# The second block's early operand is made behind the experts' additions, its weights' low halves move from GpSimd to VectorE, and its norms get a higher priority

## The chip, the cores and the metric

The kernel runs on one core of a Trainium2 chip. The metric is the device time of one execution in microseconds (us); the median of three runs of the kernel before is 1877.12 us. TensorE multiplies matrices, VectorE and ScalarE work on tiles element by element, GpSimd can do VectorE's kind of work too, and DMAs are issued from SyncE's and GpSimd's queues. In the profile these are PE (with PEld for its weight loads), DVE, ACT, POOL and SP.

## The reference

Two transformer blocks follow each other on 256 tokens of width 1024. The first one ends with a mixture of experts and an RMS norm:

```python
x = x + mod[:, 5] * _expert_choice_ffn(h2, ...)      # 16 experts, 32 tokens each
return _rmsnorm(x, final_norm_w)                     # its result is the second block's x
```

The second block has two layers. A context of 256 tokens runs beside x and gives it keys and values. Per layer of x:

```python
hx = modulate(rms_norm(x, norm1_g[l]), mod_x[0], mod_x[1])
zx = jnp.split(hx @ w_in[l], 10, axis=-1)            # ten parts of width 256 feed four mixers
x = x + mod_x[2] * token_mixers(zx, ...)             # convolution, attention, gating; then w_out
x = x + mod_x[5] * channel_mixer(modulate(rms_norm(x, norm2_g[l]), mod_x[3], mod_x[4]), w1, w2)
```

At the end stands `rms_norm(x, final_g)`. Between the blocks two norms meet: the first block's last one and the first norm of layer 0. One pass gives the row factors of both.

## The kernel before, in words

All activations are kept transposed: `xT` is 128 partitions by 8 chunks of 256 tokens. Every large product is done in three passes: weight and activation are each split into a high part (`hi`, a rounded copy that ScalarE writes) and a low part (`lo`, source minus `hi`), and TensorE adds high by high, high by low and low by high. `load_half` (L280) loads half a weight chunk (128x1024) from the stream's DMA queue into a ring of 6 raw buffers and calls `split` (L267); the subtraction runs on the engine that is handed in.

A `Stream` holds what one strand of work uses: its pools, its DMA queue, and `lo`, the engine for the low halves. The context is strand `ZF` (L1512; low halves on VectorE, loads from GpSimd's queue) and runs between the experts' matmuls. The second block's x is strand `ZC` (L1537): low halves on GpSimd (`lo=G`) in the mixers' chunks, in six halves of the output projection and in the first three chunks of the channel mixer; loads on SyncE's queue.

The experts (L1095 to L1126) end with eight additions to `xT` (L1119), one for each chunk of 128 features; behind each of them, in the last group of experts, ScalarE squares the new chunk and TensorE sums the squares (L1125). Then a Newton iteration on VectorE turns the sums into four row factors, `both` (L1130 to L1135).

`Early` (L372) lets two products of a norm start before the norm's row is known. Its operand is x times the gain, split into `preh` (ScalarE, L382) and `prel` (VectorE, L383); the row factor multiplies the product when it leaves PSUM (L415), and the shift rides along in two added columns. `product` (L392) issues the second product behind the row's transposes; `rows` (L386) copies the row. `modulate` (L360) then makes the ordinary operand, `hh` and `hlo`, chunk by chunk for all later products.

`both_norms` (L1540) serves layer 0's first norm: it multiplies the gain with the first block's final norm weight, makes the early operand in pools of strand ZC, and transposes the row out of `both`. Its `rest` (L1548) modulates and also scales `xT` itself by the first block's final norm (L1552, eight instructions). The pools of strand ZC (`cb`, `cx`, `hlx`, `ct`) are opened after the experts' pools have been closed and take over their memory. The mixers (L1256) run the two early products (chunks 1 and 0 of w_in), which give `glu`; then the 31-tap convolution by products of 32x32 (`pconv`, L1335), keys (`pk`), values (`pvv`), the query, attention in five units, and the other chunks (`zin`). `row_params` (L1141) loads the gating rows that the mixers need at L1415.

The other norms of x go through `norm` (L1487): the early operand, then `rms_rows` (L346), which squares each chunk on ScalarE (L336), adds the squares on VectorE (`acc`, L338), sums over the partitions on TensorE (L341) and runs the Newton iteration. The final norm (L1566, L1567) scales `xT` into `yo` on ScalarE and takes `rms_rows` of `xT`.

**What sets the order.** A planner orders each engine's instructions by priority (the order in the program, unless a block asks for a high priority, as `urgent`, L318, does for the Newton iteration and the row's transposes) among those that are ready by its own estimate of the time. SyncE's queue alone keeps the program's order. [...]

Of the kernel before, what the change touches and what calls it, by code (L numbers as in the profile page):

```python
# [10 lines left out]
FT = mybir.dt.float32  # L11
# [4 lines left out]
OP = mybir.AluOpType  # L16
# [9 lines left out]
RW = 1408  # L26
# [162 lines left out]
class Stream:  # L189


    def __init__(self, **kw):
        self.__dict__.update(kw)

# [11 lines left out]
def build(tc, I, out, dbg=None, upto=99):  # L206
# [22 lines left out]
    def P(n, i=0, w=None):  # L229
        o, ww = PAR[n]  # L230
        return par[:, o + i:o + (ww if w is None else i + w)]
# [113 lines left out]

    def rms_rows(Z, xt):  # L346

        return rows_of(Z, rms_of(Z, xt))

    last_row = [None]  # L350

    @urgent
    def rows_of(Z, r):

        row = Z.ms.tile([128, 512], FT, name="rrow", tag="ms")
        for a in range(2):
            last_row[0] = PE.transpose(row[:, a * 128:(a + 1) * 128], r[:, a:a + 1].to_broadcast([128, 128]), ident)  # L357
        return row[:, :T]
# [72 lines left out]
    def mod_gain(pool, mod, m, i, norm, name):  # L431
        g = pool.tile([128, 8], FT, name=name)
        V.scalar_tensor_tensor(g, mod[:, m, i * 8:i * 8 + 8], 1.0, norm, op0=OP.add, op1=OP.mult)
        return g
# [705 lines left out]

    def row_params(Z, l):  # L1141
        r = Z.big.tile([128, NROW], FT, name="rows", tag="rows", bufs=1)
        Z.dma.dma_start(r, I["rows"][l])
        return r

    def lam_of(Z, l):
# [38 lines left out]
    def v_chunk(Z, l, H, vd):  # L1185
        parts = load_split(Z, I[f"wi2_{l}"][4], Z.lo)
        ps = Z.mm.tile([128, 2, 256], FT, name="pvv", tag="mm")
        dense(ps, parts, H, True)
        evac(vd, ps)
# [66 lines left out]
    def mixers(Z, l, H, x):  # L1256
# [125 lines left out]
        if not x:  # L1382
            taps(8, 16)
        v_chunk(Z, l, H, kvd[1])
        if not x:
            taps(16, 24)
        ps = chunk(2)
# [105 lines left out]
        early.rows(row)  # L1493
        return [early, lambda: modulate(Z, xt, gain, shift, row)]

    def layer(Z, l, mod, m, x, norm1=norm):
        g1 = mod_gain(Z.h, mod, m, 1, P(f"n1_{l}"), "g1")
        H = norm1(Z, Z.x, g1, mod[:, m, 0:8], x and Z.y or None)
        Y = mixers(Z, l, H, x)
        g2 = mod_gain(Z.big, mod, m, 4, P(f"n2_{l}"), "g2")  # L1500
        out_proj(Z, I[f"wo2_{l}"], Y, mod[:, m, 16:24], eng=Z.lo, wide=x)
        H = norm(Z, Z.x, g2, mod[:, m, 24:32], x and Z.hid or None)
        mlp(Z, l, H, mod[:, m, 40:48])
# [18 lines left out]
    v_chunk(ZF, 1, H, vc[1])  # L1522
    assert not turns
    phF.close()
    phB.close()
    if upto < 6:
        return [es, es2]


    phC = ExitStack()  # L1530
    cb = phC.enter_context(tc.tile_pool(name="cb", bufs=2))
    cx = phC.enter_context(tc.tile_pool(name="cx", bufs=1))
    hlx = phC.enter_context(tc.tile_pool(name="hlx", bufs=2))
    ct_ = phC.enter_context(tc.tile_pool(name="ct", bufs=3))
    cms = phC.enter_context(tc.tile_pool(name="cms", bufs=2, space=PSUM))
    csc = phC.enter_context(tc.tile_pool(name="csc", bufs=4, space=PSUM))
    ZC = Stream(fills=1, sq="sq", raw=ringp, rawn=RW, dma=nc.sync, acc=dict(tag="hn", bufs=1), hl=itertools.cycle([hlp, hlp, hlp, hlx, hlx]), mm=fmm, ms=cms, tmp=ct_, h=cx, big=cb, hid=((cx, "hidh"), (cx, "hidl")), y=((pz, "cT"), (cx, "yl")),  # L1537
                x=xT, np=4, ahead=1, lo=G, fill=0, sc=csc, sct="sc")

    def both_norms(Z, xt, gain, shift, places):  # L1540

        gain2 = Z.h.tile([128, 8], FT, name="gain2")
        V.tensor_mul(gain2, gain, P("fn"))
        early = Early(Z, xt, gain2, shift, places)
        row = rows_of(Z, both[:, 2:4])
        early.rows(row)

        def rest():  # L1548
            H = modulate(Z, xt, gain2, shift, row)
            row1 = rows_of(Z, both[:, 0:2])  # L1550
            for k in range(KD):
                V.scalar_tensor_tensor(xt[:, k, :], xt[:, k, :], P("fn", k, 1), row1, op0=OP.mult, op1=OP.mult)  # L1552
            return H

        return [early, rest]

    for _ in range(3):
        wait = fr.tile([128, 1024], FT, name="raw", tag="raw")
# [33 lines left out]
```

## Time and profile before

| | us |
|---|---|
| runs of the kernel before | 1870.72, 1877.12, 1877.19 |
| median | 1877.12 |
| the profiled execution's own time | 1875.34 |
| its span in the trace | 1873.5 |

The profile shows one execution. Times in the trace count from the start of the span. [...] A list of waits names for each idle stretch what ended it. A line such as `acc<-acc,sq` names the tile that an instruction writes and those that it reads.

### The profile page before, as it was taken

The numbers are of one execution on the slowest core, as the hardware profiler recorded it, in microseconds if no ns is written. First come the engines' busy times: TensorE is split into PE (matmuls) and PEld (weight loads), VectorE is DVE, ScalarE is ACT, GpSimd is POOL, SyncE is SP. The second block draws the span as 40 slices with busy tenths as digits, with TensorE's granted clock in tenths as the row PEclk, the third lists the DMA queues.
The fourth block names the chain that finished last, engine by engine and source line by source line (L and its number), as shares of the span: only waits on it lengthen the run. The fifth ranks groups of instructions, "written<-read, shape, count | busy, mean of one in ns | idle before, by whom it ended". The sixth has DMA issues, their size and how long they took to land. (4 is left out here: it accounts for less than half of the span.)

```text
span 1873.5 us, 37088 instructions
## 1 busy us (share of the span) xinstructions
PE 1663.8 (89%) x15731; PEld 1327.5 (71%) x15731; DVE 992.2 (53%) x1824; ACT 626.8 (33%) x987; POOL 340.1 (18%) x348
## 2 busy tenths in 40 slices
PE   5999999787988888888887887799999999999997
PEld 3777876454665466555764565688999997789997
DVE  5666565464533432223322341656788874967564
ACT  3432332321221221112211221344554453546443
POOL 2334141200000000000000001343311136430000
PEclk7999999888898999889998989888899999999999
DMA  9666887799899999999999998432488853235561
GB/s 372 214 225 223 333 273 275 280 404 396 305 385 403 407 398 412 397 413 409 412 406 411 406 391 309 140 113 68 129 295 299 289 173 126 86 106 191 182 188 59
DMA packets 124228, 529.32 MB, mean 283 GB/s; under 512 B 13917, under 2 KB 14173, under 8 KB 123550
## 3 DMA queue, kind: packets, MB, share of 16 engines
q1 hardware_dynamic: 91086, 405.56, 57.1%
q0 software_dynamic: 32544, 119.16, 18.2%
q8 instruction: 123, 2.02, 0.4%
q10 hardware_dynamic: 432, 2.23, 0.3%
q14 instruction: 43, 0.35, 0.1%
HBM read 525.84 MB, written 1.05 MB: 281 GB/s over the span
## 5 line engine op out<-in xcount | busy, mean ns | idle before, releaser
L269 ACT ACTIVATE hi<-raw 128x1024 fp32r<-128x1024 f32 x316 | 333.0, 1057 | 743.8 <-PE oproj L312 258.6
L271 DVE TENSOR_TENSOR lo<-raw,hi 128x1024 fp32r<-128x1024 f32 x250 | 306.9, 1230 | 407.0 <-ACT hi L269 392.7
L312 PE MATMUL oproj<-hidh,hi 128*128 128x256 f32 x768 | 223.4, 291 | 3.0 <-DVE xT L911 2.9
L312 PE MATMUL oproj<-hidh,lo 128*128 128x256 f32 x768 | 221.3, 288 | 0.0
L312 PE MATMUL oproj<-hidl,hi 128*128 128x256 f32 x768 | 220.8, 288 | 0.0
L271 POOL TENSOR_TENSOR lo<-raw,hi 128x1024 fp32r<-128x1024 f32 x66 | 160.1, 2436 | 314.0 <-ACT hi L269 254.9
L312 PE MATMUL pw<-hh,hi 128*128 128x256 f32 x704 | 204.6, 294 | 2.7 <-ACT hh L367 2.3
L312 PE MATMUL pw<-hh,lo 128*128 128x256 f32 x704 | 200.0, 286 | 0.0
L312 PE MATMUL pw<-hlo,hi 128*128 128x256 f32 x704 | 195.1, 288 | 1.1 <-DVE hlo L368 1.1
L312 PEld LDWEIGHTS oproj<-hidh,hi 128*128 128x128 f32 x768 | 149.8, 195 | 19.1 <-issue 15.0
L312 PEld LDWEIGHTS pw<-hh,hi 128*128 128x128 f32 x704 | 136.8, 195 | 26.8 <-issue 20.9
L312 PEld LDWEIGHTS oproj<-hidh,lo 128*128 128x128 f32 x768 | 149.2, 194 | 5.2 <-issue 5.2
L312 PEld LDWEIGHTS oproj<-hidl,hi 128*128 128x128 f32 x768 | 149.5, 195 | 3.9 <-issue 3.9
L1065 PE MATMUL pu<-raw,xe 128*32 128x352 f32 x1024 | 108.7, 514 | 36.3 <-DMA raw<-in_wu_dram 34.7
L1065 PE MATMUL pg<-raw,xe 128*32 128x352 f32 x1024 | 106.8, 511 | 35.7 <-DMA raw<-in_wg_dram 35.4
L312 PEld LDWEIGHTS pw<-hh,lo 128*128 128x128 f32 x704 | 136.7, 194 | 1.6 <-issue 1.5
L312 PEld LDWEIGHTS pw<-hlo,hi 128*128 128x128 f32 x704 | 133.7, 195 | 5.8 <-issue 4.4
L1112 PE MATMUL pd<-raw,ht 128*32 128x128 f32 x2816 | 109.8, 281 | 20.2 <-DMA raw<-in_wd_dram 18.8
L487 DVE CUSTOM_DVE_ANT_0 raw<-raw,adarow,par 128x1024 f32<-128x1024 f32 x64 | 85.1, 1331 | 61.0 <-DMA raw<-in_ada0x_dram 41.8
L277 POOL DMA_DIRECT2D raw<-in_w_dram x64 | 33.9, 530 | 430.3 <-DVE lo L271 430.3
L1112 PEld LDWEIGHTS pd<-raw,ht 128*32 128x32 f32 x2816 | 79.1, 111 | 43.9 <-DMA raw<-in_wd_dram 22.5
L312 PE MATMUL zin<-hh,hi 128*128 128x256 f32 x272 | 85.1, 314 | 0.8 <-ACT hh L367 0.8
(459 smaller groups left out, 3363.1 us busy)
## 6 DMA issues: line engine op xcount, KB each, us to landing
raw<-in_wg_dram SPq DMA_DIRECT2D x128, 704.0 KB, 10.0
raw<-in_wu_dram SPq DMA_DIRECT2D x128, 704.0 KB, 10.3
raw<-in_wd_dram SPq DMA_DIRECT2D x128, 704.0 KB, 9.0
raw<-in_w_dram SPq DMA_DIRECT2D x128, 512.0 KB, 4.2
raw<-in_wi_dram SPq DMA_DIRECT2D x68, 512.0 KB, 5.2
raw<-in_ada_dram POOLq DMA_DIRECT2D x64, 512.0 KB, 4.9
raw<-in_w_dram POOLq DMA_DIRECT2D x64, 512.0 KB, 7.9
raw<-in_ada0x_dram POOLq DMA_DIRECT2D x32, 512.0 KB, 5.1
```

Of the source, the lines that this page charges most:

```text
L269: A.activation(hi, src, AF.Copy, scale=scale)
L271: (eng or V).tensor_sub(lo, src, hi.bitcast(FT))
L277: Z.dma.dma_start(raw[:p, :n], src)
L312: PE.matmul(ps[:, b, :], l, r, start=(n == 0), stop=(n == 47), skip_group_check=True)
L487: V.tensor_tensor_reduce(raw, raw, row, 1.0, bias[:, 16 + n:17 + n], OP.mult, OP.add, accum_out=mod[:, 0, 16 + n:17 + n])
L1065: mm = PE.matmul(ps[32 * j:32 * j + 32, :], xe[:, k, e * 32:(e + 1) * 32], raw[:, j * 352:(j + 1) * 352], start=(k == 0), stop=(k == KD - 1))
L1112: mm = PE.matmul(py[32 * j:32 * j + 32, :], hts[j][:, i, :], raw[:, n % 11 * 128:(n % 11 + 1) * 128], start=(i == 0), stop=(i == 10))
```

## The change

- **Early operand.** Layer 0's gain (`gain2`) and `Early` are made right after the context strand, before the experts' pools are closed. The high part goes where the context's x was (`pz`, tag `cT`), the low part to a new pool, `ce`, on the other side of memory. So each chunk's instructions can run as soon as the experts' addition to that chunk is done.
- **PSUM.** Two `passed` tiles are taken from the pool `csc` first, so that the first early product gets its third and fourth bank.
- **Scaling of xT.** `rest` becomes `finish`, put off until behind `v_chunk` of layer 0: the second row's transposes and the eight scalings.
- **Low halves.** Strand ZC gets `lo=V`.
- **Rows.** `row_params` issues its DMA from GpSimd's queue for both strands (`G` instead of `Z.dma`).
- **Square sums.** With `urgent=True` on strand ZC, `rms_rows` runs `rms_of` at high priority: squares, additions, sums and Newton iteration of layer 0's second norm, both norms of layer 1 and the final norm.

```diff
--- before.py
+++ after.py
@@ -189,6 +189,8 @@
 class Stream:
 
 
+    urgent = False
+
     def __init__(self, **kw):
         self.__dict__.update(kw)
 
@@ -345,7 +347,7 @@
 
     def rms_rows(Z, xt):
 
-        return rows_of(Z, rms_of(Z, xt))
+        return rows_of(Z, (urgent(rms_of) if Z.urgent else rms_of)(Z, xt))
 
     last_row = [None]
 
@@ -1140,7 +1142,7 @@
 
     def row_params(Z, l):
         r = Z.big.tile([128, NROW], FT, name="rows", tag="rows", bufs=1)
-        Z.dma.dma_start(r, I["rows"][l])
+        G.dma_start(r, I["rows"][l])
         return r
 
     def lam_of(Z, l):
@@ -1382,6 +1384,8 @@
         if not x:
             taps(8, 16)
         v_chunk(Z, l, H, kvd[1])
+        if x and Z.later:
+            Z.later.pop()()
         if not x:
             taps(16, 24)
         ps = chunk(2)
@@ -1493,9 +1497,12 @@
         early.rows(row)
         return [early, lambda: modulate(Z, xt, gain, shift, row)]
 
-    def layer(Z, l, mod, m, x, norm1=norm):
-        g1 = mod_gain(Z.h, mod, m, 1, P(f"n1_{l}"), "g1")
-        H = norm1(Z, Z.x, g1, mod[:, m, 0:8], x and Z.y or None)
+    def layer(Z, l, mod, m, x, norm1=None):
+        if norm1:
+            H = norm1()
+        else:
+            g1 = mod_gain(Z.h, mod, m, 1, P(f"n1_{l}"), "g1")
+            H = norm(Z, Z.x, g1, mod[:, m, 0:8], x and Z.y or None)
         Y = mixers(Z, l, H, x)
         g2 = mod_gain(Z.big, mod, m, 4, P(f"n2_{l}"), "g2")
         out_proj(Z, I[f"wo2_{l}"], Y, mod[:, m, 16:24], eng=Z.lo, wide=x)
@@ -1522,37 +1529,43 @@
     v_chunk(ZF, 1, H, vc[1])
     assert not turns
     phF.close()
+
+    phC = ExitStack()
+    ce = phC.enter_context(tc.tile_pool(name="ce", bufs=1, side="right"))
+    gain2 = mod_gain(pz, mods[1], 0, 1, P("n1_0"), "gain2")
+    V.tensor_mul(gain2, gain2, P("fn"))
+    early = Early(None, xT, gain2, mods[1][:, 0, 0:8], ((pz, "cT"), (ce, "yl")))
     phB.close()
     if upto < 6:
         return [es, es2]
 
 
-    phC = ExitStack()
     cb = phC.enter_context(tc.tile_pool(name="cb", bufs=2))
     cx = phC.enter_context(tc.tile_pool(name="cx", bufs=1))
     hlx = phC.enter_context(tc.tile_pool(name="hlx", bufs=2))
     ct_ = phC.enter_context(tc.tile_pool(name="ct", bufs=3))
     cms = phC.enter_context(tc.tile_pool(name="cms", bufs=2, space=PSUM))
     csc = phC.enter_context(tc.tile_pool(name="csc", bufs=4, space=PSUM))
-    ZC = Stream(fills=1, sq="sq", raw=ringp, rawn=RW, dma=nc.sync, acc=dict(tag="hn", bufs=1), hl=itertools.cycle([hlp, hlp, hlp, hlx, hlx]), mm=fmm, ms=cms, tmp=ct_, h=cx, big=cb, hid=((cx, "hidh"), (cx, "hidl")), y=((pz, "cT"), (cx, "yl")),
-                x=xT, np=4, ahead=1, lo=G, fill=0, sc=csc, sct="sc")
-
-    def both_norms(Z, xt, gain, shift, places):
-
-        gain2 = Z.h.tile([128, 8], FT, name="gain2")
-        V.tensor_mul(gain2, gain, P("fn"))
-        early = Early(Z, xt, gain2, shift, places)
-        row = rows_of(Z, both[:, 2:4])
+    ZC = Stream(fills=1, sq="sq", raw=ringp, rawn=RW, dma=nc.sync, acc=dict(tag="hn", bufs=1), hl=itertools.cycle([hlp, hlp, hlp, hlx, hlx]), mm=fmm, ms=cms, tmp=ct_, h=cx, big=cb, hid=((cx, "hidh"), (cx, "hidl")), y=((pz, "cT"), (ce, "yl")),
+                x=xT, urgent=True, np=4, ahead=1, lo=V, fill=0, sc=csc, sct="sc", later=[])
+
+
+    for _ in range(2):
+        csc.tile([128, 512], FT, name="passed", tag="sc")
+
+    def both_norms():
+
+        early.Z = ZC
+        row = rows_of(ZC, both[:, 2:4])
         early.rows(row)
 
-        def rest():
-            H = modulate(Z, xt, gain2, shift, row)
-            row1 = rows_of(Z, both[:, 0:2])
+        def finish():
+            row1 = rows_of(ZC, both[:, 0:2])
             for k in range(KD):
-                V.scalar_tensor_tensor(xt[:, k, :], xt[:, k, :], P("fn", k, 1), row1, op0=OP.mult, op1=OP.mult)
-            return H
-
-        return [early, rest]
+                V.scalar_tensor_tensor(xT[:, k, :], xT[:, k, :], P("fn", k, 1), row1, op0=OP.mult, op1=OP.mult)
+
+        ZC.later.append(finish)
+        return [early, lambda: modulate(ZC, xT, gain2, mods[1][:, 0, 0:8], row)]
 
     for _ in range(3):
         wait = fr.tile([128, 1024], FT, name="raw", tag="raw")
```

## Rows read from the trace of the kernel before

**Rows 1.** The page, busy time of each engine over the span.

```profile
PE 1663.8 (89%) x15731; PEld 1327.5 (71%) x15731; DVE 992.2 (53%) x1824; ACT 626.8 (33%) x987; POOL 340.1 (18%) x348
```

**Rows 2.** Windows: span of time and its length, busy time of each engine, granted clock, DMA share.

```profile
1168.50:1176.00 7.50, 0.00 (x0) 0.00 (x0) 6.94 (x14) 0.00 (x0) 5.41 (x3) 0.50 0.00 0
1190.00:1202.00 12.00, 7.21 (x57) 6.37 (x59) 12.00 (x28) 6.26 (x11) 4.73 (x2) 0.95 0.35 114
1331.00:1346.00 15.00, 12.09 (x63) 11.46 (x63) 9.04 (x24) 6.38 (x12) 4.75 (x2) 0.66 0.23 71
1526.00:1548.00 22.00, 19.98 (x151) 19.42 (x151) 17.28 (x37) 11.59 (x21) 9.69 (x5) 0.92 0.26 84
1670.00:1685.00 15.00, 11.80 (x67) 11.24 (x68) 9.22 (x24) 6.38 (x12) 4.76 (x2) 0.77 0.22 71
1240.40:1282.20 41.80, 41.80 (x178) 32.17 (x178) 27.85 (x69) 15.35 (x34) 12.34 (x7) 0.63 0.20 63
1590.60:1620.00 29.40, 29.40 (x179) 23.33 (x179) 27.37 (x68) 15.17 (x33) 10.14 (x5) 0.94 0.24 77
1585.00:1645.00 60.00, 57.52 (x382) 46.50 (x381) 52.05 (x104) 31.71 (x63) 26.94 (x13) 0.97 0.32 102
```

**Rows 3.** Waits of PE from 1166 to 1203: total, times, longest.

```profile
PE pk L312 <- DVE hlo L368: 4.8, 3, 2.1
PE sums L1125 <- ACT sq L1123: 2.0, 1, 2.0
```

**Rows 4.** Timeline of ACT at the passage between the blocks: start, duration, idle before.

```profile
1176.56 3.31 ACT L382 ACTIVATE preh<-xT,gain 128x256 fp32r<-128x256 f32 x8 [8.20 <-DVE gain L1543]
```

**Rows 5.** Timeline of DVE at the same passage.

```profile
1169.37 2.26 DVE L1133 SCALAR_TENSOR_TENSOR nwtv<-nwtv 128x2 f32<-128x2 f32 x1
...
1173.97 0.16 DVE L256 TENSOR_TENSOR nwta<-nwty 128x4 f32<-128x4 f32 x1
...
1200.83 0.87 DVE L1300 SCALAR_TENSOR_TENSOR glu<-aval,bias,mixh 128x256 f32<-128x256 f32 x2
...
1214.40 0.69 DVE L619 COPY mixl<-pconv 128x512 f32<-128x512 f32 x1 [11.99 <-PE pconv L1335]
```

**Rows 6.** Groups of DVE from 1168 to 1203: count, busy us, mean ns.

```profile
L368 DVE SCALAR_TENSOR_TENSOR hlo<-sq,mod,hh 128x256 fp32r<-128x256 f32 x8 | 8.3, 1070 | 0.5 <-ACT hh L367 0.5
L1552 DVE SCALAR_TENSOR_TENSOR xT<-xT,par,rrow 128x256 f32<-128x256 f32 x8 | 3.6, 471 | 0.0
```

**Rows 7.** Timeline of the SP queue at the same passage.

```profile
1176.00 0.33 SPq L1143 DMA_DIRECT2D rows<-in_rows_dram  x1
```

**Rows 8.** The page, the low halves on VectorE and on GpSimd.

```profile
L271 DVE TENSOR_TENSOR lo<-raw,hi 128x1024 fp32r<-128x1024 f32 x250 | 306.9, 1230 | 407.0 <-ACT hi L269 392.7
...
L271 POOL TENSOR_TENSOR lo<-raw,hi 128x1024 fp32r<-128x1024 f32 x66 | 160.1, 2436 | 314.0 <-ACT hi L269 254.9
```

**Rows 9.** Groups of POOL from 1585 to 1645, layer 1's attention.

```profile
L271 POOL TENSOR_TENSOR lo<-raw,hi 128x1024 fp32r<-128x1024 f32 x11 | 26.4, 2408 | 26.6 <-ACT hi L269 14.7 <-PE zin L312 11.8
```

**Rows 10.** Groups of DVE from 1585 to 1645.

```profile
L1219 DVE TENSOR_SCALAR prob<-prob,m 128x512 f32<-128x512 f32 x8 | 10.0, 1249 | 0.4
L1220 DVE SCALAR_TENSOR_TENSOR prob<-prob,m 128x512 f32<-128x512 f32 x8 | 6.0, 744 | 0.2
L1368 DVE SCALAR_TENSOR_TENSOR ya<-yth,ya 128x512 f32<-128x512 f32 x1 | 2.8, 2842 | 0.0
```

**Rows 11.** Timeline of DVE, one such instruction alone.

```profile
1244.90 0.49 DVE L1219 TENSOR_SCALAR prob<-prob,m 128x512 f32<-128x512 f32 x1
```

**Rows 12.** Timeline of DVE ahead of layer 0's second norm.

```profile
1328.21 2.61 DVE L338 TENSOR_TENSOR acc<-acc,sq 128x256 f32<-128x256 f32 x1
...
1331.92 0.41 DVE L338 TENSOR_TENSOR acc<-acc,sq 128x256 f32<-128x256 f32 x1
```

**Rows 13.** Timeline of ACT at the final norm.

```profile
1862.37 0.51 ACT L1566 ACTIVATE yo<-xT,par 128x256 f32<-128x256 f32 x1 [4.21 <-DVE xT L911]
...
1863.48 0.40 ACT L336 ACTIVATE sq<-xT 128x256 f32<-128x256 f32 x1
```

## The prediction, made before the changed kernel ran

> **What bounds the kernel now.** I read the page's busy times first, then windows around every norm of the second block, then the waits and timelines in those windows. TensorE is busy for 89% of the span, VectorE for 53%, GpSimd for 18% [rows 1]. So a change to x's strand can only pay where TensorE stands still or runs at its lower clock. The windows show where. Between the blocks TensorE does nothing from 1168.5 to 1176.0 us, and from 1190 to 1202 it works for 7.21 of 12 us while VectorE is busy all the time [rows 2]. At layer 0's second norm (1331 to 1346) it is idle for 2.9 us and its granted clock is 0.66; at layer 1's second norm (1670 to 1685) 3.2 us and 0.77; at layer 1's first norm (1526 to 1548) 2.0 us and 0.92 [rows 2]. In attention TensorE is always busy, but layer 0's stretch of 41.8 us has a clock of 0.63, and layer 1's same work (from the first scores to the convolution's row) takes 29.4 us at 0.94 [rows 2].
>
> The waits at the passage name two causes: the keys' product waits 4.8 us for `hlo`, and the last sums wait 2.0 us for a square [rows 3]. The timelines say why nothing runs before 1176: all eight `preh` start at 1176.56, 8.20 us after ScalarE fell idle, because the gain came so late [rows 4]. VectorE meanwhile is in the Newton iteration, where an instruction of two columns takes 2.26 us, beside 0.16 for its neighbours [rows 5]; GpSimd is busy for 5.41 of those 7.5 us [rows 2], so I read the long one, and the one after it that is as long, as held up by a GpSimd subtraction (2.4 us each [rows 8]).
>
> **The early operand.** Removed from the passage: the eight `preh` on ScalarE and eight `prel` on VectorE, except the last chunk's pair. They go behind the additions, in front of which VectorE waits for the experts' products. If that cover failed, the last pair alone would cost about 0.9 us. The first early product does not need the row. It can follow the last sums at 1168.5 instead of half a microsecond behind the first `preh`, at 1177: 8.5 us on TensorE. VectorE gives a second count, because `glu` (done at 1201.7 [rows 5]) releases the convolution. Its work from 1168.5 loses the scalings of `xT`, 3.6 us [rows 6], and the `prel`, eight of the same form and size, so as much again; `hlo` goes from 1.07 to the 0.47 of the scaling [rows 6], 8 x 0.6 = 4.8; the Newton iteration loses 2 x 2.1 = 4.2. That is 16.2. It gains six low halves (two early chunks, the keys) at 1.23 [rows 8], 7.4, of which perhaps two fit in ahead of 1168.5: a net of 8.8 to 11.3. I take **10 us**. From below: if VectorE takes all six ahead of the row and `hlo` gets no faster, 16.2 - 4.8 - 7.4 = 4; from above, 8.5 plus the waits for `hlo`, 4.8: 13.
>
> **What is moved with it.** The scalings land behind the values' product, where VectorE waits 11.99 us for the convolution [rows 5]; `xT` is next read at the output projection, so I cost them at nothing, and at 3.6 if that wait goes. Two of the row's transposes go with them; they are moved, not added. The `rows` DMA leaves SyncE's queue, where it waited until 1176.00 for the experts' memory with all further weight loads behind it [rows 7]; these can now start some 7 us earlier, which the earlier keys' product needs. On GpSimd's queue it has nothing behind it but the gating multiplications, its own readers. In layer 1 it follows the 32 ada loads, done in the channel mixer. Nothing either way. The two `passed` tiles only remove a possible wait for the experts' banks: nothing.
>
> **Low halves.** GpSimd has 66 of them [rows 8]; two belong to the first block, so 64 move, 32 in each layer. On VectorE one takes 1.23 us, on GpSimd 2.44 [rows 8]. In layer 1's attention 11 move [rows 9]: 13.5 us more on a VectorE that is busy 52.05 of 60 us [rows 2]. Given back: eight scalings of `prob` that take 1.25 us on average [rows 10] and 0.49 alone [rows 11], 6.1 us, and one instruction of 2.84 us whose form takes 0.74 elsewhere [rows 10], 2.1. That is 8.2 shown, and smaller groups must hold a little more, so VectorE ends between 54 and 57 of 60: it still fits. But each low half is now queued with the softmax. I charge **2 us a layer, 4 in all**; from below -2 (they come sooner), from above see the slower rival.
>
> **The norms' square sums.** At 1328.21 an addition of `acc` takes 2.61 us, a later one 0.41 [rows 12], and the next update of `xT`, which TensorE waits for, is behind it. Both causes go: GpSimd no longer subtracts there, and squares come first. What could be won at the three norms is idle time plus half of the time at 1.2 GHz: 2.9 + 5.1, 3.2 + 3.5, 2.0 + 1.8, in sum 18.5. Two low halves take 2.5 us of VectorE at each of them against some 4.4 of slowed additions, so I take half, **9 us**, with 0 and 18 as ends. At the final norm ScalarE makes `yo` before each square; the last square starts at 1863.48 [rows 13], and with both `yo` behind it, it would start some 0.7 us earlier, all of it on the path: **0.7 us**.
>
> **Sum.** 1875.34 - 10 - 9 - 0.7 + 4 = 1859.6, say **1859 us**. That is against the profiled execution's own time, whose span is 1873.5; the median of the runs is 1877.12, 1.8 above it, and one run was at 1870.72. I take 0.5%, 9.4 us, as what a measurement of this kernel can tell from no change.
>
> **Rivals.** *TensorE's clock in attention.* Layer 0's stretch took 12.4 us longer than layer 1's with the same matrix work [rows 2]. If the shift takes the low clock away there: 1859.6 - 12.4 = 1847. If layer 1 falls into it too: 1872. The two layers' difference shows that either can happen; the three runs' 6.5 us of spread speak for it also. [...] I give 0.20 to the first and 0.12 to the second.
>
> *The order doesn't change.* The planner places the products by its own estimate. If it keeps the first product behind the row's transposes, the passage gains only the Newton iteration's 4.2 us, and squares that it thought ready anyway gain half of 9: 1875.3 - 4.2 - 4.5 - 0.7 + 4 = 1870. Against it: the first product's operand is ready before the row by any estimate. 0.15.
>
> *VectorE holds up TensorE: slower.* Each low half now waits in VectorE's list behind reductions that wait for scores, and TensorE's next chunk waits for the low half. The gains of 19.7 us are used up once 16 of the 64 low halves hold TensorE up for their 1.23 us; with half of them, 1875.3 - 19.7 + 39.4 = 1895. For it: VectorE's 52.05 of 60, and the last sums' wait, where a square stood behind weight splits [rows 3]. Against it: 97% of full clock and 57.52 of 60 busy show that TensorE is served well there, with weights made several chunks ahead. [...] 0.10.
>
> **The numbers.** The forecast keeps 0.43. Faster by over 0.5% is under 1867.7: the forecast, the full clock in layer 0, and a quarter of the two cases at 1870 and 1872, 0.70. Within it the rest of those two, 0.20; slower 0.10. The range takes in 1847 and 1872 and the forecast's own bounds (with 4 and 0 for passage and norms 1875, with 13 and 18 for both 1848), and below 1847 about half of what the norms may give beyond the 9: 1842 to 1875.
>
> **What would show it.** Right: the first early product starts before 1170 on TensorE, ahead of the row; no VectorE instruction of two columns takes 2 us; the convolution starts near 1192; the windows at the three norms have less idle time and a clock above 0.8; squares ahead of `yo` at the end. Wrong: products still behind the row, or a list of waits in which TensorE waits for `lo` or `prob` in attention by more than 10 us, or VectorE full in every window there.

## The result, and the profile after

| | us |
|---|---|
| runs of the changed kernel | 1835.05, 1841.66, 1844.32, 1845.36, 1862.08 |
| their median | 1844.32 |
| the kernel before, five runs beside them | 1864.65 to 1877.19, median 1873.97 |
| ratio, 95% interval | 0.9864 [0.9819, 0.991] |
| the profiled execution, its span | 1862.08, 1860.3 |

The changed kernel is faster, by 1873.97 x 0.0136 = 25 us (17 to 34 by the interval). The prediction said 1859 us, between 1842 and 1875, and "faster"; the median lies in that range, near its lower end. The prediction had set its sum against a profiled execution of 1875.34 us: a gain of 15.7.

The profiled execution is the slowest of the five, and its clock is the lowest. TensorE's mean granted clock in the five runs, from the fastest to the slowest, is 0.944, 0.935, 0.934, 0.933 and 0.925. So the trace is read by stages, each cut at the same two instructions in both kernels, and beside each length stands its time at half clock: 2 x (1 - granted clock) x length (taken from the clock before rounding; the rounded one gives it to within half a us). That counts two clocks, as the traces show them: of the 1873 windows of 1 us in before's trace 1564 read 1.00, 241 read 0.50 and 68 something between (of the changed kernel's 1860: 1538, 241 and 81). A granted clock of 0.50 is what the prediction and the expectations call 1.2 GHz; no run here measures it as a frequency.

From the page of the changed kernel, busy times and the low halves [rows 1, 8]; GpSimd has none left in the group list:

```profile
PE 1660.5 (89%) x15731; PEld 1327.2 (71%) x15731; DVE 999.4 (54%) x1888; ACT 627.3 (34%) x987; POOL 185.6 (10%) x286
...
L273 DVE TENSOR_TENSOR lo<-raw,hi 128x1024 fp32r<-128x1024 f32 x314 | 387.8, 1237 | 448.7 <-ACT hi L271 424.9
```

64 low halves have moved (250 to 314), and VectorE's busy time grew by 7 us, not by 64 x 1.23 = 79: other instructions of VectorE got shorter (`prob` and `ya` are named below).

**The passage.** TensorE's timeline of the changed kernel: first early product, last sums, the row out of `both`, first convolution product.

```profile
1159.18 0.58 PE L412 MATMUL early<-preh,hi 128*128 128x258 f32 x1 [0.58 <-DVE xT L1121]
...
1163.36 0.50 PE L1127 MATMUL sums<-fn,sq 128*128 128x2 f32 x4
...
1166.86 0.40 PE L359 MATMUL rrow<-cst,both 128*128 128x128 f32 x2
...
1180.12 6.24 PE L1337 MATMUL pconv<-glu,dg 32*32 32x256 f32 x255
```

The early product does not merely follow the last sums: it starts 4.7 us ahead of their end at 1163.86, just after the last addition to `xT` is done (1159.12), and it fills the Newton iteration. ScalarE's last square is ready at 1160.02, but 23 of the product's 48 matmuls stand ahead of the sums in TensorE's list:

```profile
1159.62 0.40 ACT L1125 ACTIVATE sq<-xT 128x256 f32<-128x256 f32 x1
```

VectorE's timeline there [rows 5]:

```profile
1158.64 0.48 DVE L1121 SCALAR_TENSOR_TENSOR xT<-pd,mod,xT 128x256 f32<-128x256 f32 x1 [0.22 <-PE pd L1120]
...
1163.97 0.16 DVE L1132 TENSOR_SCALAR nwtv<-sums 128x4 f32<-128x4 f32 x1
...
1164.37 0.16 DVE L1135 SCALAR_TENSOR_TENSOR nwtv<-nwtv 128x2 f32<-128x2 f32 x1
...
1166.55 0.17 DVE L1137 COPY both<-nwty 128x4 f32<-128x4 f32 x1
...
1178.48 0.86 DVE L1302 SCALAR_TENSOR_TENSOR glu<-aval,bias,mixh 128x256 f32<-128x256 f32 x2
...
1196.09 0.69 DVE L621 COPY mixl<-pconv 128x512 f32<-128x512 f32 x1 [8.45 <-PE pconv L1337]
...
1207.77 3.22 DVE L1565 SCALAR_TENSOR_TENSOR xT<-xT,par,rrow 128x256 f32<-128x256 f32 x8
```

The iteration takes 1166.72 - 1163.97 = 2.75 us, and its instruction that took 2.26 us takes 0.16. `glu` is done 15.5 us after the sums (1179.34; before: 1201.69 - 1168.48 = 33.2). The scalings stand behind the values' product, as planned.

The sums themselves have moved, though. In the kernel before the last addition is done at 1166.00 and the sums 2.5 us behind it; here they come 4.7 us behind it.

```profile
1165.52 0.48 DVE L1119 SCALAR_TENSOR_TENSOR xT<-pd,mod,xT 128x256 f32<-128x256 f32 x1 [8.37 <-PE pd L1118]
```

So a stretch that starts at the last sums has lost 2.3 us at its front by the change alone. The end of the last addition, which waits for the experts' product in both kernels, is the fairer start: behind it `glu` is done after 20.2 us (before: 35.7).

**Stages.** Windows of the kernel before: last sums to first scores; layer 0's and layer 1's second norm (last output-projection product to first w2 product); layer 1's first norm (last w2 product to first scores).

```profile
1168.48:1240.45 71.97, 58.32 (x837) 50.61 (x836) 39.92 (x89) 25.90 (x43) 36.05 (x16) 0.89 0.43 142
1328.91:1386.07 57.16, 53.46 (x407) 52.19 (x406) 46.92 (x84) 31.54 (x50) 9.62 (x9) 0.91 0.58 194
1667.67:1724.93 57.26, 51.87 (x399) 50.49 (x398) 43.66 (x76) 30.92 (x49) 6.43 (x3) 0.94 0.47 154
...
1528.47:1590.61 62.14, 57.92 (x847) 50.09 (x846) 30.38 (x57) 24.30 (x39) 32.91 (x14) 0.97 0.36 116
```

The same four stages of the changed kernel, then its two attention stretches (first scores to first output-projection product):

```profile
1163.86:1223.25 59.39, 54.50 (x815) 46.20 (x814) 38.03 (x91) 21.38 (x33) 0.53 (x1) 0.94 0.41 138
...
1311.35:1367.16 55.81, 50.71 (x407) 49.61 (x407) 47.65 (x90) 33.28 (x54) 3.68 (x7) 0.94 0.61 205
1656.41:1711.89 55.48, 50.38 (x398) 49.29 (x398) 44.25 (x81) 32.37 (x53) 0.00 (x0) 0.94 0.52 166
1511.28:1569.66 58.38, 55.67 (x848) 48.28 (x847) 36.17 (x69) 23.66 (x38) 0.00 (x0) 1.00 0.37 119
...
1223.25:1287.05 63.80, 60.09 (x324) 46.22 (x323) 45.82 (x110) 29.29 (x59) 3.18 (x3) 0.79 0.24 76
1569.66:1632.12 62.46, 58.21 (x324) 45.04 (x323) 46.44 (x108) 29.08 (x59) 3.62 (x2) 0.81 0.24 76
```

From the last sums the passage is 12.6 us shorter, from the last addition 10.3 (74.4 to 64.1); the three norms are shorter by 1.4, 1.8 and 3.8. Attention shows 0.79 and 0.81 of full clock: 2 x 0.21 x 63.8 = 27 us and 24 us at half clock. That hides a part of the gain in this one execution.

### The profile page after: what moved, and what is told of

It reads as the page before. It is cut to its first block, busy times and chain, and to the rows that moved or that the text cites. A ratio compares the mean times of both kernels' runs of the same rounds, so it can differ in the third digit from the quotient of the medians.

```text
span 1860.3 us, 37102 instructions
## 1 busy us (share of the span) xinstructions
PE 1660.5 (89%) x15731; PEld 1327.2 (71%) x15731; DVE 999.4 (54%) x1888; ACT 627.3 (34%) x987; POOL 185.6 (10%) x286
## 4 chain that ended last, share of the span: by engine, by line
PE 64%; DMA 21%; DVE 7%; issue 5%; ACT 2%; POOL 1%; SPq 0%; DVEq 0%; ACTq 0%; POOLq 0%
PE oproj L314 15%; PE pw L314 11%; PE zin L314 7%; DMA raw<-in_wu_dram 7%; DMA raw<-in_wg_dram 6%; PE proj L314 6%; DMA raw<-in_wd_dram 3%; PE pd L1114 3%; PE pu L1067 3%; DMA raw<-in_ada_dram 2%; PE pg L1067 2%; PE psc L1206 2%; PE adaps L455 2%; DMA raw<-in_wi_dram 2%; PE early L412 1%
## 5 line engine op out<-in xcount | busy, mean ns | idle before, releaser
L273 DVE TENSOR_TENSOR lo<-raw,hi 128x1024 fp32r<-128x1024 f32 x314 | 387.8, 1237 | 448.7 <-ACT hi L271 424.9
L314 PEld LDWEIGHTS pw<-hh,hi 128*128 128x128 f32 x704 | 137.8, 196 | 24.6 <-issue 21.2
L1067 PE MATMUL pg<-raw,xe 128*32 128x352 f32 x1024 | 101.7, 493 | 33.8 <-DMA raw<-in_wg_dram 32.8
L1067 PEld LDWEIGHTS pu<-raw,xe 128*32 128x32 f32 x1024 | 22.8, 111 | 86.9 <-DMA raw<-in_wu_dram 62.0
L314 PE MATMUL zin<-hh,lo 128*128 128x256 f32 x272 | 82.2, 304 | 0.0
```

The costliest lines, as they stand in the source:

```text
L273: (eng or V).tensor_sub(lo, src, hi.bitcast(FT))
L314: PE.matmul(ps[:, b, :], l, r, start=(n == 0), stop=(n == 47), skip_group_check=True)
L1067: mm = PE.matmul(ps[32 * j:32 * j + 32, :], xe[:, k, e * 32:(e + 1) * 32], raw[:, j * 352:(j + 1) * 352], start=(k == 0), stop=(k == KD - 1))
```

## The experiments

Each kernel is timed against the kernel before on the same chip, and has one profile. Both kernels were run once more under new names, so that one profile need not speak for a kernel. The intervals reach 0.003 to 0.005 to either side, so two ratios can be told apart from about 0.006 on. The stages, in us, by landmark instructions; in brackets the time at half clock:

```
                          before  before  after  after  a_low   a_op.  b_low   b_sums a_sums a_scale a_rows a_second
                                  again          again  gpsimd  late   vector  first  plain  now     sync   free
last addition to scores    74.44   73.62  64.13  61.02  66.47   65.38  70.21   73.79  61.38  64.66   64.09  66.93
 of it to end of sums       2.48    1.93   4.74   4.82   3.08    2.27   1.95    1.96   3.43   3.42    3.43   6.01
 of it to end of glu       35.69   34.79  20.21  20.24  24.64   25.32  30.54   34.83  20.43  21.65   20.15  21.21
sums end to first scores   71.96   71.69  59.39  56.20  63.38   63.11  68.26   71.82  57.95  61.24   60.66  60.91
 of it to end of glu       33.21   32.86  15.48  15.42  21.56   23.05  28.60   32.87  17.00  18.23   16.72  15.19
second norm, layer 0       57.16   57.09  55.81  55.74  53.98   56.04  57.61   56.10  58.41  55.73   56.19  56.83
second norm, layer 1       57.26   55.48  55.49  55.50  55.09   55.93  58.33   55.30  58.19  55.49   55.50  57.33
first norm, layer 1        62.13   62.07  58.38  59.48  58.53   58.42  61.50   59.03  59.39  59.05   59.22  61.41
channel mixer, layer 0    142.40  142.38 144.13 143.50 145.46  144.68 139.45  142.77 143.79 141.03  152.34 146.06
last w2 to the end         11.73   11.66  11.62  11.59  11.53   11.60  11.74   11.40  11.94  11.61   11.41  11.89
attention, layer 0         63.86   54.00  63.80  53.96  61.29   65.96  65.61   55.06  54.46  54.82   55.82  64.15
 at half clock             (30.7)  (6.8)  (27.3) (3.4)  (23.9)  (34.1) (30.7)  (10.2) (6.8)  (6.8)   (6.8)  (27.3)
attention, layer 1         52.47   56.67  62.46  54.71  57.22   61.04  62.68   51.25  62.51  54.36   53.70  55.50
 at half clock             (3.4)   (13.7) (23.9) (6.8)  (13.7)  (20.5) (23.9)  (3.4)  (23.9) (6.8)   (6.8)  (6.8)
```

The edit of a_sums does not touch the passage. So three profiles show what the same passage does from one execution to the next: 61.0 to 64.1 us from the last addition to the first scores, and 20.2 to 20.4 to the end of `glu`. In one profile, then, a difference of under 3 us at the scores says nothing; `glu` is the finer measure, and the start at the last sums is left aside below.

**The two kernels once more.** No edit.

> The kernel before unchanged, for a second trace of it. Every theory: ratio 1 within 0.4%. What the trace is for: the stretch from the first scores to the output projection takes 50 us in each layer plus half of the time that it spends at 1.2 GHz, whatever that time is here; and the passage from the last sums to the convolution stays at 33 us.

> The changed kernel unchanged, for a second trace and more times. Every theory: ratio between 0.982 and 0.991. Theory 4 (VectorE's low halves make attention fall to 1.2 GHz more often): over 15 us at 1.2 GHz in each layer's attention again. Theory 5 (chance alone decides): may be anything from 3 to 34 us, as in the traces so far.

Measured: before_again 0.9974 [0.9939, 1.0009] against its own code, 1869.35 us; after_again 0.9876 [0.9832, 0.9921], 1850.10 us. The gain stands. The attention stretches of before, of before_again, and then of after_again:

```profile
1240.45:1304.31 63.86, 62.32 (x327) 48.66 (x326) 46.38 (x102) 28.62 (x59) 22.55 (x11) 0.76 0.23 73
1590.61:1643.08 52.47, 49.99 (x326) 39.78 (x326) 47.79 (x100) 28.54 (x59) 22.41 (x11) 0.97 0.28 90
```

```profile
1237.16:1291.15 53.99, 51.50 (x326) 40.68 (x325) 47.88 (x102) 28.64 (x59) 22.38 (x11) 0.94 0.27 86
1577.30:1633.97 56.67, 54.69 (x326) 42.93 (x326) 48.22 (x100) 28.65 (x59) 22.48 (x11) 0.88 0.26 84
```

```profile
1222.83:1276.79 53.96, 49.79 (x324) 39.19 (x324) 45.54 (x110) 29.20 (x59) 3.17 (x3) 0.97 0.29 89
1559.80:1614.51 54.71, 50.47 (x325) 39.50 (x324) 46.32 (x108) 28.99 (x59) 3.62 (x2) 0.94 0.27 87
```

The same code that had clocks of 0.76 and 0.97 before, and 0.79 and 0.81 after, here has 0.94 and 0.88, and 0.97 and 0.94. So the clock in attention is not fixed by the kernel. Take half of the time at half clock off each length, and the four stretches of before come to 48.5, 50.8, 50.6 and 49.8 us, those of after to 50.1, 50.5, 52.3 and 51.3: some 1.1 us a layer longer. The half is an estimate, as if all work took twice as long there: in the changed kernel's first early product the matmuls follow each other every 0.215 us at a clock of 0.50 (1159.77 to 1161.92) and every 0.118 us at 1.00 (1164.05 to 1164.76).

**Attention's low halves back on GpSimd**, in the changed kernel (in the second kernel those of the output projection and the channel mixer too, so that VectorE keeps them in the passage alone):

```diff
-        parts = load_split(Z, wi[i], Z.lo)
+        parts = load_split(Z, wi[i], G if x else Z.lo)
```

> The changed kernel with the low halves of the query's and the five later chunks (12 in each layer) back on GpSimd; the early products, keys, values, output projection and channel mixer stay on VectorE. Theory 4: under 15 us at 1.2 GHz in each layer's attention, so 5 to 12 us faster than the changed kernel by the median. Theory 5: within 3 us of it.

> As the last, and the six low halves of the output projection and the six of the channel mixer in each layer are back on GpSimd too, so that VectorE has them for the early products, keys and values alone. Adding up the stages of the traces so far: the passage keeps its 12 us, the second norms gain another 1 us each; theory 4: 7 to 14 us faster than the changed kernel; theory 5: 0 to 4 us faster.

Measured: 0.9898 [0.9849, 0.9947] and 0.9897 [0.9845, 0.9949]; neither can be told from after_again's 0.9876. The first one's attention stretches:

```profile
1227.95:1297.48 69.53, 65.18 (x327) 50.55 (x326) 46.81 (x107) 28.96 (x59) 11.91 (x7) 0.73 0.22 72
1578.55:1627.76 49.21, 47.37 (x326) 38.09 (x325) 43.67 (x105) 28.05 (x59) 11.24 (x6) 0.97 0.29 93
```

With low halves on GpSimd the clock was 0.73 in one layer and 0.97 in the other. Over all profiles, the sixteen stretches with attention's low halves on VectorE spent 16.4 us at half clock on average, the twelve with them on GpSimd 14.5. That low halves on VectorE bring the low clock (theory 4 in the expectations) has fallen; that it comes by chance from execution to execution (theory 5) is what is left. Why it falls where it does stays open.

**Low halves alone, added to before and taken from after** (the two edits side by side, each line cut to the part that differs).

```diff
 b_low_vector (kernel before)             a_low_gpsimd (kernel after)
-  np=4, ahead=1, lo=G,                   -  urgent=True, np=4, ahead=1, lo=V,
+  np=4, ahead=1, lo=V,                   +  urgent=True, np=4, ahead=1, lo=G,
```

> The kernel before with one part alone: strand ZC's low halves on VectorE. Theory 1 (the passage gains by the early operand's place, the low halves relieve the norms): the Newton iteration behind the experts takes about 3 us instead of 7.5, TensorE starts the first early product some 4 us earlier, the three norms between 4 and 9 us less in sum; 8 to 13 us faster by the median. Theory 2 (the low halves on GpSimd were the whole trouble): nearly all of the change's gain, 20 us or more. Theory 3 (the change's gain is mostly the clock's doing in attention): within 6 us of the kernel before, and the stretches at 1.2 GHz in attention explain its time.

> The changed kernel with strand ZC's low halves back on GpSimd. Theory 1: loses what the low halves gave: 8 to 12 us slower than the changed kernel (ratio to the kernel before about 0.992), the Newton iteration back to 7 us, but the first early product still starts ahead of the row. Theory 2: 20 us slower than the changed kernel, ratio near 0.998.

Measured: 0.9953 [0.9919, 0.9987], and 0.9906 [0.9869, 0.9943]. Alone, the low halves bring `glu` 4.7 us forward (30.5 against a mean of 35.2), shorten the passage by 3.8 us (70.2 against 74.0) and lengthen the second norms by 2.4 (57.61 + 58.33 = 115.9 against a mean of 113.5 for the pair). Taken away, they cost 4.4 us at `glu` (24.6 against 20.2), and the second norms get 2.2 shorter. In the runs 0.9906 cannot be told from after_again's 0.9876, so what the low halves earn in the whole program is small or nothing that is shown. VectorE's timeline of a_low_gpsimd shows where they help:

```profile
1157.72 0.16 DVE L1132 TENSOR_SCALAR nwtv<-sums 128x4 f32<-128x4 f32 x1
1157.91 2.12 DVE L1134 TENSOR_SCALAR nwtv<-nwtv 128x2 f32<-128x2 f32 x1
1160.07 2.30 DVE L1135 SCALAR_TENSOR_TENSOR nwtv<-nwtv 128x2 f32<-128x2 f32 x1
1162.40 2.27 DVE L256 TENSOR_SCALAR nwty<-nwtv 128x4 int32<-128x4 int32 x1
1164.70 0.16 DVE L258 TENSOR_TENSOR nwta<-nwty 128x4 f32<-128x4 f32 x1
```

And GpSimd's timeline of the same kernel:

```profile
1152.74 11.89 POOL L273 TENSOR_TENSOR lo<-raw,hi 128x1024 fp32r<-128x1024 f32 x5 [69.23 <-ACT hi L271]
```

Five subtractions run end to end until 1164.63. Until then three instructions of two or four columns take 2.1 to 2.3 us each; the one ahead of them, which reads the sums that TensorE left in PSUM, takes 0.16, and from 1164.70 on each takes 0.16. Now TensorE waits 5.4 us for `both`. In the trace of after, with no subtraction on GpSimd there, the same three take 0.16 to 0.17 us each. So each of the three lasts about as long as one subtraction beside it (11.89 us for five, 2.4 each). Two of them (L1134, L256) read a single tile; what holds them up beside a subtraction no run here shows.

**The early operand made late again** (changed kernel, `gain2` and `Early` in `both_norms`, behind the closing of the experts' pools):

```diff
-    gain2 = mod_gain(pz, mods[1], 0, 1, P("n1_0"), "gain2")
-    V.tensor_mul(gain2, gain2, P("fn"))
-    early = Early(None, xT, gain2, mods[1][:, 0, 0:8], ((pz, "cT"), (ce, "yl")))
     phB.close()
...
     def both_norms():
-        early.Z = ZC
+        gain2 = mod_gain(ZC.h, mods[1], 0, 1, P("n1_0"), "gain2")
+        V.tensor_mul(gain2, gain2, P("fn"))
+        early = Early(ZC, xT, gain2, mods[1][:, 0, 0:8], ((pz, "cT"), (ce, "yl")))
```

> The changed kernel with the early operand made where it was made before, in both_norms once strand ZC's pools are open; all else as changed. Theory 1: preh and prel come behind the Newton iteration again, the time from the last sums to the convolution grows from 16 to some 24 us, the whole 6 to 9 us slower than the changed kernel. Theory 2: within 3 us of the changed kernel.

Measured: 0.9942 [0.9908, 0.9976]. `glu` is done 25.3 us behind the last addition, 5.1 later than in after, and the list of TensorE's waits has one for the Newton iteration:

```profile
PE rrow L359 <- DVE both L1137: 5.0, 1, 5.0
```

The early operand is worth those 5 us at `glu`: they are the iteration that has nothing beside it otherwise. At the first scores 65.4 us against 61.0 to 64.1 leave some 3 of them.

**The square sums' priority, added to before and taken from after** (side by side; lines cut, and the default `urgent = False` left out).

```diff
 b_sums_first (kernel before)             a_sums_plain (kernel after)
-  x=xT, np=4,                            -  x=xT, urgent=True, np=4,
+  x=xT, urgent=True, np=4,               +  x=xT, np=4,
-  rows_of(Z, rms_of(Z, xt))
+  rows_of(Z, (urgent(rms_of) if Z.urgent else rms_of)(Z, xt))
```

> The kernel before with one part alone: rms_of at high priority on strand ZC. Theory 1: less than 3 us either way, of which 0.7 at the final norm; the norm windows keep their slow additions of acc (2 us and more), since GpSimd still subtracts beside them. Rival: the square sums' place is what earns the 8 us at the norms, then 5 to 9 us faster.

> The changed kernel without the high priority for the square sums. From the stages of the traces so far (the sums alone took 2 us off the second norms and 3 off layer 1's first, the low halves alone added 2.5 to the second norms): each second norm, from the output projection's last matmul to the channel mixer's second product, back from 55.6 to 57 to 58 us, layer 1's first norm from 59 to 61; 4 to 7 us slower than the changed kernel, ratio 0.990 to 0.992. If the high priority earns nothing beside VectorE's low halves: those stages within 0.5 us and the ratio as the changed kernel's.

Measured: 0.9933 [0.9904, 0.9962], and 0.9929 [0.9897, 0.996]. Against the mean of the two profiles of before, the priority takes off 1.0 us (layer 0's second norm), 1.1 (layer 1's) and 3.1 (layer 1's first norm): 5.2 in sum. Without it, the changed kernel loses 2.6, 2.7 and 0.5 at the same three places, and 0.3 at the end: 6.1. So the priority is worth 5 to 6 us in the stages in either kernel. In after, 3.1 of its 5.3 us at the second norms make up for what the rest costs there: without it they take 116.6, against 113.5 before.

**The scalings of `xT` where they were** (`finish` called inside `rest`):

```diff
-        ZC.later.append(finish)
-        return [early, lambda: modulate(ZC, xT, gain2, mods[1][:, 0, 0:8], row)]
+        def rest():
+            H = modulate(ZC, xT, gain2, mods[1][:, 0, 0:8], row)
+            finish()
+            return H
+        return [early, rest]
```

> The changed kernel with the eight scalings of xT back behind the modulation. If they cost what VectorE spends on them in the passage: 3 to 3.5 us more from the last sums to glu, and as much to the first scores, ratio 0.989 to 0.990. If the planner puts them where VectorE idles anyway: under 1 us.

Measured: 0.9912 [0.9878, 0.9947]. Five of the eight scalings, 0.46 us each, stand ahead of the end of `glu`, which comes 1.4 us later behind the last addition (21.6 against 20.2). The first scores, 64.7 us behind it, are within 0.6 us of after's slower profile, and the ratio cannot be told from after_again's. So putting the scalings off earns 1.4 us at `glu`, and more is not shown.

**The rows on SyncE's queue** (changed kernel):

```diff
-        G.dma_start(r, I["rows"][l])
+        Z.dma.dma_start(r, I["rows"][l])
```

> The changed kernel with the gating rows' DMA back on SyncE's queue. If the weights behind it in SyncE's queue are what the earlier keys' product waits for: the rows' DMA goes out only when the experts' memory is free, the keys' weights land several us later, and the passage to the first scores grows by 4 to 8 us over 57.8. If not: within 1 us, as my prediction had it for either place.

Measured: 0.9935 [0.9899, 0.9972]. SyncE's queue in this kernel:

```profile
1161.51 7.23 SPq L279 DMA_DIRECT2D raw<-in_wi_dram  x4
1179.58 0.33 SPq L1145 DMA_DIRECT2D rows<-in_rows_dram  x1
1179.96 17.10 SPq L279 DMA_DIRECT2D raw<-in_wi_dram  x10
```

In the profile of after_again nothing stands between the weight loads:

```profile
1148.31 50.23 SPq L279 DMA_DIRECT2D raw<-in_wi_dram  x16
```

On SyncE's queue the rows wait, and ten weight loads with them, until 1179.96. But behind the last addition `glu` comes after 20.2 us and the first scores after 64.1, as in after: the keys' product waits 1.3 us for a weight's `hi`, and 1.8 for `hlo` in after. That the rows' place earns anything in the passage is not shown; the ratio, 0.006 above after_again's, is at the edge of what the runs can tell. This profile's experts ended late (last sums at 1176.5 us; the other thirteen 1157.7 to 1170.4), and their last weight loads had started late already, at 1095.6 us against 1082.1 and 1084.7 in the two profiles of after, ahead of the rows in the queue. Its layer 0 channel mixer took 152.3 us, which I can't explain from the edit.

**The second early product let go of the row's transposes** (changed kernel). In after TensorE waits 6.8 us for `nwty`; the edit was to fill that.

```diff
-            if self.n > 1:
+            if self.n > 2:
```

> The changed kernel without the rule that the second early product is issued behind the row's transposes (for all four norms of x). TensorE waits for the Newton iteration at rrow 7.3 us in sum in the changed kernel's trace; if the planner lets the second product fill these waits, they fall under 3 us and the stages of the three later norms get 1 to 2 us shorter each, ratio 0.984 or less. If the planner then puts the row behind the whole second product, modulation starts up to 6 us later and the stages get longer by 1 to 3 us each.

Measured: 0.997 [0.9935, 1.0004]: most of the gain of the whole change is lost again. From its list of TensorE's waits from 1150 to 1870, and then from the changed kernel's:

```profile
PE rrow L359 <- DVE nwty L260: 10.7, 3, 4.3
```

```profile
PE rrow L359 <- DVE nwty L260: 6.8, 3, 2.3
```

The wait grew. TensorE's timeline at layer 0's second norm in this kernel:

```profile
1322.29 3.04 PE L412 MATMUL early<-prel,hi 128*128 128x258 f32 x24
1325.17 0.50 PE L343 MATMUL rms<-cst,acc 128*128 128x1 f32 x4
1325.53 1.03 PE L343 MATMUL rms<-cst,sq 128*128 128x1 f32 x8
1330.81 0.66 PE L359 MATMUL rrow<-cst,nwty 128*128 128x128 f32 x2 [4.25 <-DVE nwty L260]
```

The second product is over when the squares are summed, so the iteration has nothing beside it. Against the mean of after the second norms take 2.9 us more in sum, layer 1's first norm 2.5 and the passage 4.4. The rule that holds the second product back (`issue_after`) is worth about 1%: 0.0094 between the ratios, with 0.006 either way.

No version tried is shown to beat the changed kernel.

## Why the prediction was right, by its own steps

**The passage: predicted -10 (4 to 13), measured -10.3 and -12.6, a mean of -11.5.** These are the two pairs of profiles, from the end of the last addition. The mechanism held, and so did the size. TensorE is idle for 15.1 and 14.5 us of before's stretch and for 4.9 and 3.2 of after's: -10.2 and -11.3, nearly all of it. "It can follow the last sums" fell short, because the product goes ahead of them: its start moved forward by 11.0 us, counted from the last addition, where the step had 8.5. But the sums come later for it, and from them alone the stage would look 14.0 us shorter. The count over VectorE (8.8 to 11.3) was too small: `glu` comes 15.0 us sooner, and the convolution starts at 1180.1 instead of near 1192 as named (6.9 us of that are this execution's earlier last addition). Only two low halves (1171.65 and 1175.69) stand between the sums and `glu`, where the count had four to six, and `mixh` on VectorE (L1298), 2.32 us in before, takes 0.41. By parts, each taken from after alone and measured at `glu`: early operand 5.1, low halves 4.4, scalings 1.4, rows nothing. They sum to 10.9 of the 15.0; the rest belongs to none of them alone.

**Moved steps: predicted 0, and nothing else is shown.** Where the scalings went they cost nothing: VectorE still waits 8.45 us for the convolution ahead of them. What they free was counted over VectorE as 3.6; taken back alone they cost 1.4, as only five of them then stand ahead of `glu`. The rows were costed as "nothing either way", and nothing more is shown for them. One detail of that step was wrong without effect: in layer 1 the rows go out at 1285.14, well ahead of the ada loads and not behind them.

**Norms: predicted -9 (0 to 18), measured -5.4.** The mean of before is 175.6 us for all three (57.1, 56.4, 62.1), of after 170.2 (55.8, 55.5, 58.9). The step that failed is "two low halves take 2.5 us of VectorE against some 4.4 of slowed additions": the additions did become short (0.42 us), but at layer 0's second norm five low halves, 6.1 us, stand on VectorE between the last product and the Newton iteration, in spite of the additions' priority, and alone the low halves lengthen the second norms by 2.4 us. Two lines of VectorE's timeline there:

```profile
1318.95 1.23 DVE L273 TENSOR_TENSOR lo<-raw,hi 128x1024 fp32r<-128x1024 f32 x1
1320.08 0.89 DVE L340 TENSOR_TENSOR acc<-acc,sq 128x256 f32<-128x256 f32 x2
```

The iteration starts 11.3 us behind the last product (1322.62), in before 11.7 (1340.61). The prediction's own windows [rows 2], placed as far behind the last product, in the changed kernel:

```profile
1313.44:1328.44 15.00, 9.97 (x61) 9.13 (x62) 12.84 (x34) 7.44 (x17) 0.00 (x0) 0.81 0.55 176
1508.81:1530.81 22.00, 22.00 (x255) 21.38 (x265) 18.76 (x50) 10.84 (x20) 0.00 (x0) 1.00 0.36 118
1658.74:1673.74 15.00, 10.22 (x61) 9.37 (x62) 12.70 (x34) 7.31 (x16) 0.00 (x0) 0.79 0.59 176
```

At layer 1's first norm TensorE now never stands still: right. At the second norms it is idle for 5.0 and 4.8 us instead of 2.9 and 3.2, at a higher clock (0.81 and 0.79), and VectorE is busy for 12.8 us instead of 9: the sign that was named, less idle time, came out wrong there. The time at half clock in these windows (the prediction's 1.2 GHz, a frequency that no run here shows; shown is the granted clock of 0.50) fell from 2 x 0.34 x 15 = 10.2 us to 5.7 (layer 1: 6.9 to 6.3); the idle part had been costed, that it could grow had not.

**Final norm: predicted -0.7, measured -0.1.** ScalarE's timeline at the end [rows 13]:

```profile
1849.29 0.42 ACT L338 ACTIVATE sq<-xT 128x256 f32<-128x256 f32 x1 [4.62 <-DVE xT L913]
1849.61 0.49 ACT L1579 ACTIVATE yo<-xT,par 128x256 f32<-128x256 f32 x1
1850.01 0.40 ACT L338 ACTIVATE sq<-xT 128x256 f32<-128x256 f32 x1
```

One `yo` still stands between the two squares, so the last square gained half of what was said; the Newton iteration starts 1.52 us behind the last update instead of 1.86, and the stretch from the last multiplications to the end took 6.28 us instead of 6.05 (6.26 and 6.05 in the second profiles), for a reason that stays open.

**Low halves in attention: predicted +4, measured about +2.** With half of the low-clock time taken off, the stretches are 1.1 us a layer longer, and before's own four differ by 2.3. VectorE did not fill: 45.5 to 46.4 us busy in stretches of 54 to 64, against 46.4 to 48.2 before. The prediction's 60 us of layer 1, placed alike in after_again, say the same:

```profile
1554.19:1614.19 60.00, 55.76 (x365) 44.49 (x365) 50.80 (x114) 30.90 (x61) 3.62 (x2) 0.94 0.30 95
```

It said 54 to 57 us for VectorE there, 52.05 before; it is 50.80. The low halves brought 13.6 us, and 14.9 were given back where 8.2 had been counted. The two slowed forms came back as counted: `prob`'s scaling from 1249 ns to 483, `ya`'s addition from 2842 to 678 (after_again).

**The sum.** Passage -11.5, norms -5.4, end -0.1, output projections -0.6, layer 0's channel mixer +1.4 (not foreseen), layer 1's -0.1: -16.3. With +2.2 for attention it is -14.1, against the predicted -15.7. That the two are so near is in part luck: too much for the norms (3.6 us) was balanced by a little too little for the passage and too much charged in attention. The runs' -25, and 1.24% or 23 us of the repeat, have intervals that reach down to 17 and 15, so they hold more than the stages do. What it is stays open. The experts end 4.3 us sooner in after's two profiles (last addition), but over all fourteen that end lies between 1154.6 and 1173.0 us with no order by the change. The runs' clocks point at time at half clock: by the formula above, after_again's six runs spent 241 us at it on average, the seventeen of before beside them 278, and before_again's twelve, of the same code as those, 262. Half of the difference, the estimate of above, is 11 to 19 us of the 23, and the passage accounts for 4 of it (16.8 us at half clock against 8.3, from the last addition). Whether the change makes the low clock rarer or chance did, no run here shows.

**The rivals.** The clock rival happened in the profiled execution (both layers low, 51 us at half clock against 34 before) and not in the repeat: it deserved its chance, but in these two stretches it comes and goes without any change. "The order doesn't change" fell: the first early product ran at 1159.18. "VectorE holds up TensorE" fell: in attention TensorE waits 8.0 us in all for the softmax's `m` and `prob` (before: 2.8) and for no `lo`, under the 10 that were named; that low halves wait behind late reductions was an estimate.

## What to carry to other kernels

Where two blocks meet, make the next product's operand inside the last loop that writes its source, so that the product fills the norm's serial arithmetic (5 us at `glu` here); and keep GpSimd's subtractions out of a stretch where VectorE runs many tiny instructions in a row (here three of them took 2.1 to 2.3 us each beside the subtractions, and 0.16 to 0.17 without). Start and end a stage at instructions that the change does not move: the last sums came 2.6 us later behind the last addition, and a stage that starts with them looks that much shorter. Before a stage is compared, put its time at the lower clock aside (3.4 to 37.6 us in one stretch of attention here), and take a second profile of both kernels: the same passage differed by 3 us between two of them.

## What the runs showed of the hardware

In one program, the changed kernel, layer 0's stretch of attention spent 27 us at half clock in one execution and 3.4 in another; over all traces here such a stretch spent 3.4 to 37.6, with TensorE idle for less than 5 us of the stretch wherever its window stands above. The two executions took 63.80 and 53.96 us: 9.8 us in one layer, without any change of the program. And the runs of the changed kernel, 27 us apart, stand in the order of their granted clocks (0.944 in the fastest, 0.925 in the slowest).

Beside GpSimd's subtractions VectorE's smallest instructions paid most for their size: 0.16 us became 2.1 to 2.3, three times in a row (after and a_low_gpsimd), while a 128x256 addition went from 0.4 to 2.6 [rows 12], where before's GpSimd subtracts from 1327.98 to 1330.54.
